# The output projection of a hybrid layer, split into a half that needs mLSTM only and a half that needs attention

## The chip, the cores and the metric

The kernel runs on one core of one Trainium2 chip. A core has five engines that work side by side, each through its own instructions in a fixed order: TensorE (PE; its weight loads are listed as PEld), VectorE (DVE), ScalarE (ACT), GpSimd (POOL), and SyncE (SP), which here only issues DMAs. The metric is the device time of one execution in microseconds (us), lower is better; "before" is the median of three runs.

## The reference, cut to what matters

One layer of an encoder for 2048 + 256 tokens (two request groups, same weights), model width 1024, in float32:

```python
h = rmsnorm(x, norm1_w)
mq, mk, mv, mo, gates, aq, ak, av = split(h @ w_in)
m_out = mlstm_mixer(mq, mk, mv, mo, gates, b_gates, mh_norm_w)   # 8 heads x 64 = 512 channels
a_out = attention_mixer(aq, ak, av, q_norm_w, k_norm_w)          # 8 heads x 64 = 512 channels
x = x + concatenate([m_out, a_out], axis=-1) @ w_out             # (T, 1024) @ (1024, 1024)
h = rmsnorm(x, norm2_w)
u = centred_dwconv(h @ w_up, conv_w, conv_b)
a, g = split(u)
y = rmsnorm(x + (silu(g) * a) @ w_down, final_norm_w)
```

The line with `w_out` is the output projection. Its first 512 input channels come from mLSTM, its last 512 from attention.

## The kernel before, in words

Everything is kept transposed (channels on the 128 partitions, tokens along the free axis), so the 1024 channels are 8 chunks of 128 (`NCC = 8`); the 2304 tokens are 18 tiles of 128 or 9 blocks of 256 (`NB = 9`, `BT = 256`). float32 products are made of three matmuls: each operand is split into a rounded high part (ScalarE's Copy) and the rest (a subtraction on VectorE), and hi x hi, hi x lo, lo x hi are added up in PSUM.

Phase a computes the norm, the attention inputs and the gates. Then two generators run interleaved, `mlstm` and `attention`. Attention goes unit by unit: 512 queries of a head or of two heads against all keys. A unit's matmuls are named by their tiles: `px` (scores for the row maximum, reduced on VectorE into `mx`), `pr` (the negated maximum, spread over partitions; it needs `m` and `m4r` of VectorE), `ps` (the scores), `ph`/`pl` (hi and lo of the exponential, ScalarE and VectorE), `pv` (times the values). When a unit is done, `fin1` to `fin3` copy it out of PSUM (ScalarE), take the reciprocal of the sums (VectorE, tile `rs`), multiply (POOL, tile `o`) and store it with POOL's queue into the DRAM array `mix_d`, 64 channels at a time. fin3 comes in the middle of the next unit. Channel chunks 0 to 3 of `mix_d` come from mLSTM, chunks 4 to 7 from attention; a block's chunk 7 (heads 6 and 7) comes last.

`phase_c` is the output projection, also a generator. It first loads and splits the weights (`weights`, tile `wo`). For block b, `loads` brings the 8 chunks of `mix_d` (tiles `cmx`, split on ScalarE and VectorE) and the residual x (tiles `cx`, four of two channel chunks each). For each z of 0 to 3 `mm` fills one PSUM tile `po` (two output chunks, 8 input chunks x 3 matmuls of 256 columns each, 48 in all; two buffers), and `post` adds it to x on VectorE, stores x1 to DRAM and squares it (ScalarE, summed on POOL). `tail` of the block before, called behind the first `mm` of the next block, makes the mean of squares (tiles `rs_c`, `rcol_c`), multiplies (8 instructions on VectorE, L1020) and stores the normed block into `n2_d`.

`run_both` sets the order in which the program is written down. While mLSTM has steps left, it goes ahead of attention by a fixed ratio. When mLSTM is done, phase_c is created (`after_m`), and from then on each attention step is preceded by one step of phase_c, if the block that phase_c wants is in `g.mixed`, to which attention's fin4 adds a block when its last heads are written. When attention is done, the rest of phase_c's steps is written out between the first steps of the FFN: `n2_sums` (tiles `rn`: sums of n2_d blocks on POOL, stored to `n2t_d`) and `n2_load` (tiles `n` and `nt`, split on ScalarE and VectorE). The first of these take memory that attention used; the later ones take memory that the projection used. Then `up_start` and `phase_d`, the FFN (matmul tiles `pa`, `pb`, `pc` for the up projection, `pd` for down).

Within this order a scheduler places the instructions of each engine: it moves an instruction ahead where its operands are ready earlier in its own model of time, and gives attention's instructions a higher priority (`tc.high_priority(offset=APRI)`) once phase_c runs. Buffers of one tag are used in the order of the program, so with two `po` buffers the third group in the program waits for the first one's addition. On the chip each engine, and each DMA-issuing queue, takes its instructions strictly in the resulting order.

Of the kernel before, what the change touches and what calls it, by code (L numbers as in the profile page):

```python
# [9 lines left out]
F32 = mybir.dt.float32  # L10
F32R = mybir.dt.float32r
AF = mybir.ActivationFunctionType
ALU = mybir.AluOpType
# [4 lines left out]
P = 128  # L18
D = 1024
NCC = D // P  # L20
T1, T2 = 2048, 256
T = T1 + T2
NT = T // P
# [13 lines left out]
BT = 256  # L37
NB = T // BT
NTB = 8
CX = 8  # L40
# [3 lines left out]
WSTEP = 2  # L44
# [2 lines left out]
OW3 = 3  # L47
OTB = 3
MXB = 8
LAGO = 2  # L50
AB = 3
NH = 386
# [3 lines left out]
WB = 8  # L56
# [29 lines left out]
def f32(ap):  # L86
    return ap.bitcast(F32)
# [32 lines left out]
def rstd_bc(g, sp, pp, sqs, n, ptag, name, bufs=1):  # L120


    nc = g.nc
    k = n // P
    ps = pp.tile([P, 512], F32, tag=ptag, name="rs_" + name, bufs=bufs)
    for t in range(k):
        for i, sq in enumerate(sqs):
            nc.tensor.matmul(ps[:, 504 + 2 * t:506 + 2 * t], sq[:, t * P:(t + 1) * P], g.ones, start=i == 0,
                             stop=i == len(sqs) - 1)
    r = sp.tile([P, 4], F32, tag="rcol", name="rcol_" + name)[:, 0:k]  # L130
    nc.vector.tensor_scalar(r, ps[:, 504:504 + 2 * k].rearrange("p (t o) -> p t o", o=2)[:, :, 0], EPS, None, ALU.add)
    nc.gpsimd.tensor_tensor(r, r, g.mhalf[:, 0:k], ALU.pow)
    for t in range(k):
        nc.tensor.matmul(ps[:, t * P:(t + 1) * P], r[:, t:t + 1].to_broadcast([P, P]), g.ident, start=True, stop=True)
    return ps[:, 0:n]
# [824 lines left out]
def phase_c(g, sn, sp, pp, wps):  # L960

    nc = g.nc
    wo = []
    g.normed = set()

    def weights(c):

        wo.append([wps[c // 4].tile([P, 2, 512], F32R, tag="w", name=f"wo{c}_{k}", bufs=WB) for k in range(2)])  # L970
        for k, w in enumerate(wo[c]):
            if c < 4:
                t = g.raw.tile([P, 512], F32, tag="raw", name=f"ro{c}_{k}", bufs=2)
            else:
                t = sp.tile([P, 512], F32, tag="x", name=f"ro{c}_{k}", bufs=CX)
            split(g, w[:, 0, :], w[:, 1, :], g.w_out[0, c * P:c * P + P, 512 * k:512 * k + 512], t)

    def loads(b):
        mx = []
        x = [sp.tile([P, 2, BT], F32, tag="x", name=f"cx{b}_{z}", bufs=CX) for z in range(4)]  # L980
        for z in range(4):
            for o in range(2):
                c = 2 * z + o
                if b % 2:
                    m = sp.tile([P, 2, BT], F32R, tag="mx", name=f"cmx{b}_{c}", bufs=MXB)
                else:
                    m = sn.tile([P, 2, BT], F32R, tag="nT", name=f"cmx{b}_{c}", bufs=NTB)
                nc.sync.dma_start(f32(m[:, 1]), g.mix_d[b, :, c])
                nc.scalar.activation(m[:, 0], f32(m[:, 1]), AF.Copy)  # L989
                nc.vector.tensor_tensor(m[:, 1], f32(m[:, 1]), f32(m[:, 0]), ALU.subtract)  # L990
                mx.append(m)
        for z in range(4):
            for t in range(2):
                nc.sync.dma_start(x[z][:, :, t * P:(t + 1) * P], g.xT[2 * b + t, :, 2 * z:2 * z + 2])
        return x, mx

    def mm(b, z, mx):
        po = pp.tile([P, 2, BT], F32, tag="po", name=f"po{b}_{z}")
        for o in range(2):
            n = slice(((2 * z + o) % 4) * P, ((2 * z + o) % 4 + 1) * P)  # L1000
            for c in range(NCC):
                for k, (a, h) in enumerate(((0, 0), (0, 1), (1, 0))):
                    nc.tensor.matmul(po[:, o], wo[c][z // 2][:, a, n], mx[c][:, h, :],  # L1003
                                     start=(c == 0 and k == 0), stop=(c == NCC - 1 and k == 2))
        return po

    def post(b, z, x, po, acc):
        nc.vector.tensor_tensor(x[z], po, x[z], ALU.add)
        g.st.dma_start(g.x1_d[b, :, 2 * z:2 * z + 2], x[z])
        q = acc if z == 0 else sp.tile([P, 2, BT], F32, tag="sq", name=f"csq{b}_{z}", bufs=1)  # L1010
        nc.scalar.activation(q, x[z], AF.Square, scale=1.0 / 32.0)
        if z:
            nc.gpsimd.tensor_tensor(acc, acc, q, ALU.add)

    def tail(b, x, acc):
        nc.gpsimd.tensor_tensor(acc[:, 0], acc[:, 0], acc[:, 1], ALU.add)
        r = rstd_bc(g, sp, pp, [acc[:, 0]], BT, "r", f"c{b}")
        for z in range(4):
            for o in range(2):
                nc.vector.scalar_tensor_tensor(x[z][:, o], x[z][:, o], g.n2w[:, 2 * z + o:2 * z + o + 1],  # L1020
                                               r, ALU.mult, ALU.mult)
            g.st.dma_start(g.n2_d[:, 2 * z:2 * z + 2, b * BT:(b + 1) * BT], x[z])
        g.normed.add(b)

    for c in range(NCC):
        weights(c)
        if c % WSTEP == WSTEP - 1:
            yield None
    prev = None
    for b in range(NB):  # L1030
        yield 2 * b
        x, mx = loads(b)
        for z in range(4):
            po = mm(b, z, mx)
            if z == 0:
                if prev is not None:
                    tail(*prev)
                acc = sp.tile([P, 2, BT], F32, tag="acc", name=f"cacc{b}", bufs=1)
            post(b, z, x, po, acc)
            if z < 3:  # L1040
                yield None
        prev = (b, x, acc)
    g.c_end = lambda: tail(*prev)

# [111 lines left out]
def phase_d(g, tc, s1, pd, ops, first):  # L1156
# [5 lines left out]
    with ExitStack() as st:  # L1162
# [17 lines left out]
        for b in range(ND):  # L1180
# [70 lines left out]
            def down(nm, acts, wds, order, fin=False):  # L1251

                for (c, z0, z1) in order:
# [73 lines left out]
def body(tc, aps, phases="abcd"):  # L1327
    nc = tc.nc
    g = Ctx()
# [3 lines left out]
    with ExitStack() as st:  # L1333
# [30 lines left out]
        with ExitStack() as s2:  # L1364
# [37 lines left out]
            def after_m():  # L1402
                s_m.close()
                swo = pool(s_wo, "wo", bufs=1, side="right")
                sc = pool(s_wo, "c_s", bufs=2, side="right")
                pc = pool(s_wo, "c_p", bufs=2, space=PSUM, side="right")
                return phase_c(g, g.sn, sc, pc, (sw, swo))

            rest = run_both(g, tc, attention(g, tc, sa, sk, pa), mlstm(g, tc, g.sm, sm2, sw, g.sn, g.pj, pm), after_m)
        with ExitStack() as s2:  # L1410
            s1 = pool(s2, "d_1", bufs=2)
# [13 lines left out]
            first = [up_start(g, s1, pd, ops, 0, NFC)]  # L1425
# [8 lines left out]
def run_both(g, tc, a, m, after_m):  # L1434


    na = 32 * (8 * 2.2 + 1) + 4 * 3.2
    nm = (NT * 6 + 1) + 2 * (NT * 8.7 + 4) + (NT * 5.7 + 4) + NT * OW3
    g.mixed = set()
    c, tile_c = None, None  # L1440
    da = dm = 0.0
    while da is not None or dm is not None:
        if dm is not None and (da is None or dm * na < LEAD * da * nm):
            s = next(m, None)
            dm = None if s is None else dm + s
            if dm is None:
                c = after_m()
                tile_c = next(c)
# [68 lines left out]
```

## Time and profile before

| | |
|---|---|
| runs before | 3471.99 us median of 3 (3470.3 to 3475.37) |
| profiled execution | 3475.05 us, span 3473.3 us, mean granted TensorE clock 0.985 |
| output projection's matmuls (L1003) | 1728, the first at 1388.5 us, the last at 1872.4 us |
| end of attention's matmuls | 1814.9 us |
| FFN's first matmul | 1872.5 us |
| busy | PE 96%, PEld 89%, DVE 77%, ACT 56%, POOL 32% |

Rows of the profile begin with a time from the span's start or with a line of the kernel, then the engine, the operation, the output tiles "<-" the input tiles, and shapes; "x3" is a count, and a bracket at the end gives the idle time of the engine just before and what ended it. SPq is SyncE's queue of DMA issues. DRAM arrays lose a digit in the rows: `n2_d` is n_d and `x1_d` is x_d.

### The profile page before, as it was taken

To read this page: it belongs to the slowest core of one execution; us is meant where nothing else is said; L and a number is where in the kernel's file an instruction comes from. 1 tells how busy PE (TensorE), PEld (TensorE's weight loads), DVE (VectorE), ACT (ScalarE), POOL (GpSimd) and SP (SyncE) were. 2 spreads that over 40 slices of the span, in tenths; PEclk is the share of its full clock that TensorE was granted. 3 is DMA by queue.
4 is the path that set the end of the run, shared out by engine and by line. 5 is a ranking of instruction groups with operands and counts; after the bars stand their busy time and mean duration, and the time that the engine had idled before them with its cause. 6 is when DMAs were issued, how large, how long until landed. Compare 5 with 4: busy or idle time off the path is not lost. (4 is left out here: it accounts for less than half of the span.)

```text
span 3473.3 us, 55765 instructions
## 1 busy us (share of the span) xinstructions
PE 3346.2 (96%) x20058; PEld 3103.0 (89%) x20058; DVE 2670.5 (77%) x4654; ACT 1930.9 (56%) x4329; POOL 1103.9 (32%) x1328
## 2 busy tenths in 40 slices
PE   7989999999999999999988999999999999999998
PEld 6878888888888887987778999999999998999998
DVE  6875687677777789767666888888888878887776
ACT  4536566666666766645554444446544446555555
POOL 6643133222224322211116233225333224322222
PEclk9999999999999999999999999999999999999999
DMA  6765334343355443432218233223333223421221
GB/s 222 238 197 162 117 107 118 104 131 101 105 169 161 131 144 115 145 105 70 68 51 296 73 97 98 74 65 130 127 105 99 67 73 119 145 65 63 73 73 50
DMA packets 258501, 404.29 MB, mean 116 GB/s; under 512 B 33552, under 2 KB 158256, under 8 KB 258224
## 3 DMA queue, kind: packets, MB, share of 16 engines
q1 hardware_dynamic: 230320, 358.24, 32.3%
q0 software_dynamic: 11344, 33.04, 3.5%
q10 hardware_dynamic: 16560, 9.44, 0.9%
q8 instruction: 158, 2.59, 0.3%
q14 instruction: 119, 0.97, 0.1%
HBM read 316.73 MB, written 83.90 MB: 115 GB/s over the span
## 5 line engine op out<-in xcount | busy, mean ns | idle before, releaser
L1257 PE MATMUL pd<-act,wd 128*128 128x384 f32 (+1 forms) x3120 | 593.2, 336 | 25.2 <-DVE acc L1259 14.4
L1257 PEld LDWEIGHTS pd<-act,wd 128*128 128x128 f32 x3120 | 539.5, 189 | 34.0 <-DVE acc L1259 20.0
L586 DVE TENSOR_TENSOR pl<-ps,ph 128x512 fp32r<-128x512 f32 x520 | 354.1, 685 | 235.3 <-ACT ps L585 228.2
L1119 PE MATMUL pa<-nt,wut 128*128 128x386 f32 (+2 forms) x2376 | 454.5, 339 | 2.0 <-DVE nt L1071 2.0
L1119 PEld LDWEIGHTS pa<-nt,wut 128*128 128x128 f32 x2376 | 421.4, 190 | 2.3 <-DVE nt L1071 2.3
L584 ACT ACTIVATE ph<-ps 128x512 fp32r<-128x512 f32 x520 | 309.7, 596 | 177.1 <-PE ps L581 172.3
L558 DVE TENSOR_REDUCE mx<-px 128x1 f32<-128x512 f32 (+1 forms) x528 | 343.8, 671 | 67.4 <-PE px L557 65.4
L1213 DVE SCALAR_TENSOR_TENSOR y<-u,cw,y 128x768 f32<-128x768 f32 (+1 forms) x264 | 314.0, 1190 | 36.3 <-ACT y L1206 29.2
L598 PE MATMUL pv<-ph,v 128*128 128x512 f32 (+1 forms) x1040 | 330.2, 405 | 2.9 <-ACT ph L584 2.4
L1124 POOL TENSOR_TENSOR tw<-ru 128x512 f32<-128x512 f32 x66 | 91.1, 1380 | 744.4 <-DMA ru<-w_up 573.3
L1135 ACT ACTIVATE u<-pa 128x386 f32<-128x386 f32 (+2 forms) x264 | 128.4, 486 | 328.4 <-PE pa L1119 326.9
L585 ACT ACTIVATE ps<-ps 128x512 f32<-128x512 f32 x520 | 310.9, 599 | 0.0
L1259 DVE TENSOR_TENSOR acc<-pd,acc 128x384 f32<-128x384 f32 (+1 forms) x544 | 280.6, 536 | 34.5 <-PE pd L1257 33.5
L1003 PEld LDWEIGHTS po<-cmx,wo 128*128 128x128 f32 x1728 | 233.9, 191 | 32.6 <-ACT cmx L989 16.2
L1003 PE MATMUL po<-cmx,wo 128*128 128x256 f32 x1728 | 242.2, 284 | 14.9 <-ACT cmx L989 14.8
L580 PE MATMUL ps<-qq,kk 128*128 128x512 f32 x520 | 217.0, 421 | 1.8 <-DVE pl L586 1.1
L557 PE MATMUL px<-kk,qq 128*128 128x512 f32 (+1 forms) x528 | 207.7, 411 | 6.6 <-DVE pl L586 3.5
L598 PE MATMUL pv<-pl,v 128*128 128x512 f32 x520 | 206.6, 407 | 6.9 <-DVE pl L586 6.6
L581 PE MATMUL ps<-qm,kl 65*128 65x512 f32 x520 | 209.1, 405 | 0.0
L724 PE MATMUL mj<-mn,wm 128*128 128x256 f32 x1296 | 197.4, 288 | 3.5 <-ACT og L738 2.1
L724 PEld LDWEIGHTS mj<-mn,wm 128*128 128x128 f32 x1296 | 182.1, 192 | 17.6 <-ACT og L738 2.5
L734 PE MATMUL mv<-wm,mn 128*128 128x256 f32 x1296 | 196.2, 288 | 1.1 <-ACT qb L730 0.9
(288 smaller groups left out, 7239.0 us busy)
## 6 DMA issues: line engine op xcount, KB each, us to landing
ru<-w_up SPq DMA_DIRECT2D x132, 512.0 KB, 3.4
mn<-n_d SPq DMA_DIRECT2D x216, 256.0 KB, 3.3
rd<-w_down SPq DMA_DIRECT2D x66, 512.0 KB, 3.6
n_d<-n1T SPq DMA_DIRECT2D x18, 1024.0 KB, 5.6
dm<-nm_d POOLq DMA_DIRECT2D x72, 256.0 KB, 4.0
mjn<-n_d SPq DMA_DIRECT2D x72, 256.0 KB, 3.3
mvn<-n_d SPq DMA_DIRECT2D x72, 256.0 KB, 3.2
q_d<-qz SPq DMA_DIRECT2D x18, 512.0 KB, 3.5
```

Of the source, the lines that this page charges most:

```text
L558: nc.vector.tensor_reduce(s.mx[:, t, z0:z0 + 1], ps[:, 0:w], AX.X, ALU.max)
L580: nc.tensor.matmul(ps, kk[:, kc:kc + P], s.qq[:, 0:N], start=True, stop=False)
L584: nc.scalar.activation(ph, ps, AF.Exp)
L585: nc.scalar.activation(ps, ps, AF.Exp)
L586: nc.vector.tensor_tensor(pl, ps, f32(ph), ALU.subtract)
L598: nc.tensor.matmul(s.pv[0:HD if k in (1, 3) else P, 0:N], v, p, start=(kp == 0 and k == 0), stop=(2 * kp + 2 == s.nk and k == 5))
L724: nc.tensor.matmul(pj[:, o], s.w[c][:, a, o * P:(o + 1) * P], nT[c][:, :, h, :], start=(c + o + k == 0), stop=(c == NCC - 1 and k == 2 and ...
L1003: nc.tensor.matmul(po[:, o], wo[c][z // 2][:, a, n], mx[c][:, h, :], start=(c == 0 and k == 0), stop=(c == NCC - 1 and k == 2))
L1119: nc.tensor.matmul(p, w[:, aa, c, :], ops[k][:, c, bb, 0:n], start=c == 0 and i == 0 and not add, stop=c == NCC // 2 - 1 and i == 2, skip_ ...
L1213: nc.vector.scalar_tensor_tensor(y[:, s:e], u[:, s + k:e + k], cw[:, k, jj:jj + 1], y[:, s:e], ALU.mult, ALU.add)
L1257: nc.tensor.matmul(po, wds[j][c // 4][:, aa, c % 4 * P:(c % 4 + 1) * P], acts[j][:, bb, z0:z1], start=(j == 0 and k == 0), stop=(j == len( ...
L1259: nc.vector.tensor_tensor(accs[c][:, z0:z1], po, accs[c][:, z0:z1], ALU.add)
```

## The change

phase_c becomes two generators. `first` takes channel chunks 0 to 3 (mLSTM's): for each block and each z it loads x (tile `xp`, three buffers), makes a `po` group of 24 matmuls, adds it to x on VectorE and stores the sum into a new DRAM array `xp_d`. `second` takes chunks 4 to 7: it loads `xp_d` back as `cx`, makes a `po` group of 24 matmuls, adds and goes on as before (`post`, `tail`). At the end of phase_c a small loop chooses the program whose step is written down: `second` if its block is in `g.mixed` and `first` has done it, else `first`. `run_both` no longer looks at `g.mixed` and takes one step of this loop per attention step. The loads of a block's chunks (`mixed`) and their splits (`parts`) are separate now, and the first program's loads come half a block ahead.

```diff
-    def loads(b):
-        mx = []
-        x = [sp.tile([P, 2, BT], F32, tag="x", name=f"cx{b}_{z}", bufs=CX) for z in range(4)]
...
+    def mixed(b, c0):
+        mx = []
+        for c in range(c0, c0 + H):
+            if c0:
+                m = sp.tile([P, 2, BT], F32R, tag="mx", name=f"cmx{b}_{c}", bufs=MXB)
+            else:
+                m = sn.tile([P, 2, BT], F32R, tag="nT", name=f"cmx{b}_{c}", bufs=NTB)
+            nc.sync.dma_start(f32(m[:, 1]), g.mix_d[b, :, c])
+            mx.append(m)
+        return mx
+
+    def parts(mx):
+        for m in mx:
+            nc.scalar.activation(m[:, 0], f32(m[:, 1]), AF.Copy)
+            nc.vector.tensor_tensor(m[:, 1], f32(m[:, 1]), f32(m[:, 0]), ALU.subtract)
+
+    def mm(b, z, c0, mx):
+        po = pp.tile([P, 2, BT], F32, tag="po", name=f"po{b}_{z}_{c0}")
...
-            for c in range(NCC):
+            for c in range(H):
...
+    def first():
+        for c in range(H):
+            weights(c)
...
+        mx = mixed(0, 0)
+        parts(mx)
+        for b in range(NB):
+            for z in range(4):
+                x = sp.tile([P, 2, BT], F32, tag="xp", name=f"xp{b}_{z}", bufs=XPB)
+                for t in range(2):
+                    nc.sync.dma_start(x[:, :, t * P:(t + 1) * P], g.xT[2 * b + t, :, 2 * z:2 * z + 2])
+                po = mm(b, z, 0, mx)
+                if b + 1 < NB and z == 1:
+                    nxt = mixed(b + 1, 0)
+                if b + 1 < NB and z == 3:
+                    parts(nxt)
+                    mx = nxt
+                nc.vector.tensor_tensor(x, po, x, ALU.add)
+                g.st.dma_start(g.xp_d[b, :, 2 * z:2 * z + 2], x)
+                yield b + (z == 3)
...
+    def second():
+        for c in range(H, NCC):
+            weights(c)
...
+        prev = None
+        for b in range(NB):
+            mx = mixed(b, H)
+            x = [sp.tile([P, 2, BT], F32, tag="x", name=f"cx{b}_{z}", bufs=CX) for z in range(4)]
+            for z in range(4):
+                nc.sync.dma_start(x[z], g.xp_d[b, :, 2 * z:2 * z + 2])
+            yield b
+            parts(mx)
+            for z in range(4):
+                po = mm(b, z, H, mx)
+                if z == 0:
+                    if prev is not None:
+                        tail(*prev)
+                    acc = sp.tile([P, 2, BT], F32, tag="acc", name=f"cacc{b}", bufs=1)
+                post(b, z, x, po, acc)
+                if z < 3:
+                    yield b
+            prev = (b, x, acc)
+            g.c_end = lambda: tail(*prev)
+            yield b + 1
+
+    s1, s2 = first(), second()
+    done = b = 0
+    while b < NB:
+        if 2 * b in g.mixed and done > b:
+            b = next(s2)
+        elif done < NB:
+            done = next(s1)
+        yield
...
+        dram("xp_d", [NB, P, NCC, BT])
...
             for _ in range(CSTEP):
-                if c is not None and (tile_c is None or tile_c in g.mixed):
-                    tile_c = next(c, NT)
+                if c is not None:
+                    next(c, None)
```

More of the change, by code (lines that the diff above doesn't have):

```diff
@@ L49 @@
 MXB = 8
+XPB = 3
 LAGO = 2
@@ L964, in phase_c @@
     nc = g.nc
-    wo = []
+    wo = {}
     g.normed = set()
+    H = NCC // 2
     def weights(c):
-        wo.append([wps[c // 4].tile([P, 2, 512], F32R, tag="w", name=f"wo{c}_{k}", bufs=WB) for k in range(2)])
+        wo[c] = [wps[c // H].tile([P, 2, 512], F32R, tag="w", name=f"wo{c}_{k}", bufs=WB) for k in range(2)]
         for k, w in enumerate(wo[c]):
-            if c < 4:
+            if c < H:
                 t = g.raw.tile([P, 512], F32, tag="raw", name=f"ro{c}_{k}", bufs=2)
@@ L1005, in mm @@
-        return po
+                    nc.tensor.matmul(po[:, o], wo[c0 + c][z // 2][:, a, n], mx[c][:, h, :],
+                                     start=(c == 0 and k == 0), stop=(c == H - 1 and k == 2))
+        return po
+    def first():
+        for c in range(H):
+            weights(c)
+            if c % WSTEP == WSTEP - 1:
+                yield 0
+        mx = mixed(0, 0)
[14 more added lines that the diff above has]
+                yield b + (z == 3)
@@ L1023, in tail @@
         g.normed.add(b)
[L1025 to L1043, printed above, removed]
+    def second():
+        for c in range(H, NCC):
+            weights(c)
+            if c % WSTEP == WSTEP - 1:
+                yield 0
+        prev = None
[26 more added lines that the diff above has]
+        yield
 OPS = ("11", "21", "t2", "t1", "t3", "22", "t4")
```

22 lines of the change are left out of this document (1 added, 21 removed).

## The prediction

> **What bounds the kernel now.** I read the page first, then the stretches around the output projection, then the order of time on TensorE, VectorE and the DMA queue where a stretch shows a gap.
>
> ```profile
> span 3473.3 us, 55765 instructions
> PE 3346.2 (96%) x20058; PEld 3103.0 (89%) x20058; DVE 2670.5 (77%) x4654; ACT 1930.9 (56%) x4329; POOL 1103.9 (32%) x1328
> L1003 PE MATMUL po<-cmx,wo 128*128 128x256 f32 x1728 | 242.2, 284 | 14.9 <-ACT cmx L989 14.8
> ```
>
> TensorE (PE) is the bound, and the edit neither adds nor removes one of its 1728 projection matmuls: only PE's idle time, its clock and the waits at the two ends of the projection can change. They lie in these stretches (columns: stretch, length, busy time and count of PE, PEld, DVE, ACT, POOL; then granted clock, DMA share, GB/s):
>
> ```profile
> core 0: us, PE busy (x) PEld busy (x) DVE busy (x) ACT busy (x) POOL busy (x), PEclk, DMA share, GB/s
> 1565.18:1569.71 4.53, 0.48 (x5) 0.17 (x3) 4.44 (x12) 0.00 (x0) 0.00 (x0) 1.00 0.39 130
> 1569.71:1577.35 7.64, 7.64 (x22) 5.92 (x23) 2.67 (x4) 5.16 (x10) 0.00 (x0) 0.55 0.68 198
> 1577.35:1598.30 20.95, 18.68 (x74) 11.86 (x72) 16.94 (x27) 12.90 (x26) 2.40 (x3) 1.00 0.10 26
> 1600.00:1640.00 40.00, 40.00 (x268) 35.99 (x267) 24.79 (x42) 21.24 (x43) 6.97 (x7) 1.00 0.19 60
> 1814.90:1829.02 14.12, 0.19 (x2) 0.00 (x1) 6.52 (x13) 1.60 (x3) 2.39 (x3) 0.66 0.66 187
> 1829.02:1872.53 43.51, 43.51 (x351) 43.51 (x351) 21.40 (x30) 13.24 (x20) 32.65 (x30) 0.95 0.94 322
> ```
>
> With projection work at hand PE issues 268 matmuls in 40 us; without it 74 in 20.95 us, where VectorE (DVE) is 81% busy. So there are "gated stretches" in which attention runs alone, and at attention's end 14.1 us in which PE stands. In PE's order of time (start, duration, count):
>
> ```profile
> 1562.04 0.41 PE L1003 MATMUL po<-cmx,wo 128*128 128x256 f32 x2
> 1569.71 0.33 PE L569 MATMUL pr<-identr,m4r 128*128 128x128 f32 x1 [4.05 <-DVE m4r L566]
> 1577.58 1.10 PE L598 MATMUL pv<-ph,v 128*128 128x512 f32 x4
> 1598.32 0.50 PE L1003 MATMUL po<-cmx,wo 128*128 128x256 f32 x2 [0.30 <-ACT cmx L989]
> 1814.60 0.48 PE L598 MATMUL pv<-pl,v 128*128 128x512 f32 x1
> 1829.02 29.12 PE L1003 MATMUL po<-cmx,wo 128*128 128x256 f32 x228 [13.93 <-ACT cmx L989]
> 1862.13 10.56 PE L1003 MATMUL po<-cmx,wo 128*128 128x256 f32 x86
> 1872.53 2.29 PE L1119 MATMUL pa<-n,wu 128*128 128x386 f32 x12
> 1878.92 0.34 PE L1119 MATMUL pc<-nt,wut 128*128 128x386 f32 x1
> ```
>
> From these the issue interval of a matmul: 256 columns (10.56 - 0.28)/85 = 0.121 us, 512 columns (1.10 - 0.39)/3 = 0.237 us, 386 columns (2.29 - 0.34)/11 = 0.177 us.
>
> **The change: the order it makes.** The compiled order of both kernels is the same up to the first projection matmul and again from early in the FFN on, so 1388 to about 1960 us is all there is to cost. The two programs do not run apart there: one step of the projection is handed out per attention step, and by the time it is wanted block b's attention is always emitted, so the order alternates: first half of block 0, second half of block 0, first half of block 1, and so on to block 8. The first program is never more than one block ahead. Since both halves take their turns in the same two po buffers, two second-half groups that wait for attention's last chunk (channel chunk 7 of mix_d) hold both, and no later first half can pass them. What the order does give is 72 matmuls (the first half of one block, 96, less the 24 fewer that are issued early from the waiting second half), moved once from behind attention's end to ahead of it. There are 342 projection matmuls behind the last attention matmul before, 271 after. Counting 512-column attention matmuls between the last early projection matmul and the first that uses chunk 7, the three gated stretches (blocks 4, 5, 6) have 96, 106, 108 before and 80, 104, 108 after. Only the first shrinks.
>
> **Step 1, the gated stretch of block 4.** It lasts from 1562.3 to 1598.3, 36.0 us. Its 4.05 us gap is VectorE's:
>
> ```profile
> 1566.16 3.21 DVE L1020 SCALAR_TENSOR_TENSOR cx<-cx,nw,rs_c 128x256 f32<-128x256 f32 x8
> 1569.29 0.16 DVE L564 TENSOR_REDUCE m<-mx 128x4 f32<-128x16 f32 x1
> 1814.89 3.22 DVE L1020 SCALAR_TENSOR_TENSOR cx<-cx,nw,rs_c 128x256 f32<-128x256 f32 x8 [3.25 <-PE rs_c L134]
> 1818.03 3.37 DVE L615 RECIPROCAL rs<-rs 64x128 f32<-64x128 f32 x4
> 1877.43 1.49 DVE L1071 TENSOR_TENSOR nt<-nt 128x772 fp32r<-128x772 f32 x1
> ```
>
> The eight multiplications of block 3's tail() stand in front of the row maximum that pr waits for. In the new order they stand behind it, and some 20 projection matmuls (2.4 us) lie between the last px and pr, so I take the gap as gone, and with it the low clock after it (0.55 over 7.64 us, so 7.64 x 0.45 = 3.4 us). The new length: 72 x 0.121 = 8.7 us of moved work, 16 x 0.237 = 3.8 us for the 16 attention matmuls that now run beside it, and 80 matmuls at the gated pace of 20.95/74 = 0.283 us, 22.7 us: 35.2 us. VectorE's 3.2 us of tail work now falls into the gated part; there it has 4.0 us to spare in 20.95, so the addition is 0 to 3.2, and I take 1.6, the middle. 36.8 against 36.0: attention's end moves **+0.8** us (-0.8 to +2.4).
>
> The Trainium skill (TensorE: Matmul & The Clock Gate, Part 1) says that an idle window of about 3.4 us halves the array clock and a busy window of the same length restores it. By that the dip is half of 3.4 us, 1.7 instead of 3.4, and the saving and the sum would be 1.7 us worse; the trace's 0.55 over 7.64 us agrees with the halving, not with so short a recovery.
>
> **Step 2, the wait at attention's end.** The chain before: VectorE's tail of block 6 and then the reciprocal (rows above), POOL's product, its store to mix_d, SP's load of the chunk, its split.
>
> ```profile
> 1810.82 0.71 POOL L132 TENSOR_TENSOR rcol_c<-rcol_c,mhalf 128x2 f32<-128x2 f32 x1 [6.87 <-DVE rcol_c L131]
> 1823.08 1.14 POOL L622 DMA_DIRECT2D mix_d<-o  x2 [0.29 <-POOL o L619]
> 1826.05 0.34 SPq L988 DMA_DIRECT2D cmx<-mix_d  x1
> 1826.43 2.04 SPq L1086 DMA_DIRECT2D rn<-n_d  x4
> 1828.52 2.24 SPq L1069 DMA_DIRECT2D n<-n_d  x4
> 1872.72 1.40 SPq L1069 DMA_DIRECT2D nt<-n2t_d  x3
> rn<-n_d SPq DMA_DIRECT2D x8, 386.0 KB, 5.1
> x_d<-cx SPq DMA_DIRECT2D x9, 256.0 KB, 4.7
> ```
>
> After, the same chain with two differences. The mean's small instructions (rcol_c on VectorE, the power on POOL, two rs_c matmuls) come behind the last pl instead of ahead of it; POOL's power took 0.71 us, and for the two small steps around it I estimate 0.5, so the reciprocal starts 1.2 us later. And the eight loads (rn, n) stand ahead of the chunk's on SP, their splits ahead of its split on ScalarE and VectorE. The loads wait for PE and VectorE, not for the mix; the reload of x ahead of them waits for a store to land (4.7 us in the median of this stretch, row x_d<-cx), one that is issued a little ahead of attention's end, so by estimate they start 3.3 us behind it. They carry 8 x 386 KB = 3.16 MB, at 322 GB/s 9.8 us: done 13.1 us behind it. The chunk's load, 1826.05 - 1814.9 = 11.2 us behind attention's end before, is now at 11.2 + 1.2 = 12.4; for the 0.7 us in which the eight are still under way I add 0.6. **+1.8** us; bounds 0 (all hidden, the mean too) and 13 (second rival).
>
> **Step 3, behind the wait.** 342 matmuls took 43.5 us. After, 71 of them are gone, 8.6 us, and 16 FFN matmuls stand among the rest, 16 x 0.177 = 2.8: 37.7 us, -5.8. The 2.8 us of FFN work come to nothing: the nt loads go into memory that the last projection matmul frees (issued 1872.72, 0.2 us behind it), their split starts at 1877.43, pc at 1878.92, 6.4 us behind the projection's end; work done before then only leaves a longer wait. So **-5.8** us (-8.6 if the 2.8 do count, -3.0 if FFN's other operands, read 8.6 us sooner, are late by 2.8).
>
> **Step 4, what is added.** 36 VectorE additions at the price of this row, 36 x 0.682 = 24.6 us, and 36 stores and 36 reloads of 256 KB (36 x 0.33 + 36 x 0.46 = 28 us of SP's issue, 18.9 MB):
>
> ```profile
> L1008 DVE TENSOR_TENSOR cx<-po,cx x36: 665/682/692, 1407.2 to 1874.2; 128x512 f32<-128x512 f32 x36
> L994 SPq DMA_DIRECT2D cx<-xT x64: 367/460/1889, 1393.7 to 1732.3; - x64
> ```
>
> The cover: beside full PE work VectorE is busy 24.8 of 40 us, and the DMA engines 19%. A po group is now 24 matmuls, 2.9 us alone, and with two buffers its addition must be done within the next group's 2.9 us or PE stands. Behind a reload on SP, which waits for its store to land (that same 4.7 us), stand other reloads, xT loads and the next mix chunks, all a z-step (3 to 6 us) ahead of need; no chunk-7 load is directly behind one. Bounds 0 and 24.6; I take **+1.5**, near the lower, since the row of 1600 to 1640 has the room. Weights, splits, xT loads and squares keep their count: 0.
>
> **The sum:** 0.8 + 1.8 - 5.8 + 1.5 = -1.7 us. The profiled execution took 3475.05 us (span 3473.3 and 1.75 around it), 3.06 above the median 3471.99 of the three runs. So 3473.3 for that execution, and **3470** as a median.
>
> **The rivals.**
> No loss, a real gain (faster): the chunk is as early as before (step 2: 0), additions cost nothing (0), the FFN work counts (-8.6) and block 4's stretch takes its best (-0.8): -9.4, 3462.6. For it: the FFN's first loads start some 10 us sooner behind attention's end. Against it: the nt loads do not.
> The loads ahead of the chunk (slower): if the eight loads go only when SP gets there at 1826, because their buffers or the reload ahead of them come late, the chunk is issued 4.3 us later and lands up to 9.8 us later still, +13 in place of +1.8: 3470 + 11 = 3481. It decides from about 11 us on, in place of the 1.8. For it: ScalarE and VectorE, too, now split these loads before the chunk. The Trainium skill (DMA: Bandwidth & Descriptors, Queues, rings and completion order) says that each DMA engine takes a row's descriptors in ring order, so a late chunk would indeed wait behind all 3.16 MB. Against it: they wait for no part of the mix.
> Additions that show (slower): half of the 24.6 us comes to light as waits for a po buffer, or for a reload on SP: +11, 3481.
> The program does run ahead (faster): the 14.1 us gap and the gated stretches fill, -20 or more, 3450. The compiled order excludes it but for mistakes of mine.
>
> **How the numbers follow.** What a measurement of this kernel can tell from no change is about 0.2%, 7 us. My forecast with no more than that either way: 0.40. Faster: the real gain 0.23 and the program ahead 0.02, 0.25. Slower: loads ahead 0.17, additions 0.18, 0.35. The range: 3458 (the gain, and the execution's own scatter of some 4 us) to 3488 (a slower rival, with half of the other's price); the forecast's own is 3464 to 3478.
>
> **What would show it.** In the profile after: pr of block 4's stretch with no 4 us wait, and the granted clock near 1 there; the stretches of blocks 5 and 6 as before; a wait of po for the chunk of 14 to 17 us (14.1 before); the projection ending some 38 us behind it; the wait of pc for nt longer. Wrong if po waits for additions (VectorE or PSUM) sum to more than 5 us, if the wait for the chunk is over 20 us, or if matmuls of a later block stand in a gated stretch.

## The result, and the profile after

The changed kernel takes 3485.05 us, median of 5 runs (3484.16 to 3489.82), beside 3470.30 of the kernel before in the same series (3469.56 to 3475.37): a ratio of 1.0041, 95% interval 1.0027 to 1.0056. It is 14 us slower where 1.7 us faster, and no measurable change, was forecast. The profiled execution took 3489.82 us, the slowest of the five; the profile of the kernel before is of an execution of 3475.05 us, near the top of its range too.

The page's lines of the changed kernel:

```profile
span 3488.1 us, 55875 instructions
PE 3347.9 (96%) x20058; PEld 3097.7 (89%) x20058; DVE 2700.1 (77%) x4690; ACT 1932.0 (55%) x4329; POOL 1112.3 (32%) x1328
L1003 PE MATMUL po<-cmx,wo 128*128 128x256 f32 x1728 | 244.4, 283 | 17.2 <-ACT cmx L994 15.0
```

TensorE's busy time is the same to 2 us; the rest of the 14.8 us between the two spans is idle time. To place them I follow three marks in PE's order of time: the first projection matmul, the last attention matmul (attention's end) and the end of the span. Changed kernel, PE:

```profile
1828.89 0.40 PE L599 MATMUL pv<-pl,v 128*128 128x512 f32 x1
1844.90 0.80 PE L1003 MATMUL po<-cmx,wo 128*128 128x256 f32 x2 [15.05 <-ACT cmx L994]
1846.79 22.84 PE L1003 MATMUL po<-cmx,wo 128*128 128x256 f32 x172 [1.09 <-DVE cmx L995]
1884.21 1.59 PE L1158 MATMUL pb<-n,wu 128*128 128x386 f32 x8
1897.69 1.01 PE L129 MATMUL rs_c<-ones,cacc 128*128 128x2 f32 x4 [9.62 <-POOL cacc L1039]
```

| | before | after | difference |
|---|---|---|---|
| first projection matmul | 1388.5 | 1390.7 | +2.2 |
| from there to attention's end (1815.1, 1829.3) | 426.6 | 438.6 | +12.0 |
| from there to the end of the span | 1658.2 | 1658.8 | +0.6 |

The 2.2 us lie where both orders are the same; the first projection matmul of the kernels below scatters from 1384.0 to 1393.1 us, without a pattern. So nearly all of the loss is in the 427 us in which attention and projection share TensorE, and behind attention's end, where 71 projection matmuls (8.6 us) were taken away, nothing was won. The stretch from the first projection matmul to attention's end, before and then after (columns as in the prediction):

```profile
1388.50:1815.10 426.60, 408.64 (x2443) 346.01 (x2441) 293.07 (x515) 235.59 (x464) 64.65 (x68) 0.98 0.28 85
1390.70:1829.30 438.60, 418.25 (x2512) 351.72 (x2511) 313.00 (x542) 235.21 (x460) 63.88 (x68) 0.98 0.39 121
```

Most of the 12.0 us are busy time of TensorE, as the profile models it, 9.6 us more, of which the 71 moved matmuls are 8.6; idle time grew by 2.4. So the moved work was paid ahead of attention's end and not hidden there. Behind it TensorE is busy 7.3 us less and idle 7.9 us more, and its waits from attention's end to 1960 us show for what. Changed kernel (engine, line, what it waited for, us in total, times, longest):

```profile
PE po L1003 <- ACT cmx L994: 15.0, 1, 15.0
PE rs_c L129 <- POOL cacc L1039: 9.6, 1, 9.6
PE po L1003 <- DVE cmx L995: 1.1, 1, 1.1
PE pc L1158 <- ACT u L1174: 0.7, 1, 0.7
```

The kernel before, from 1814 us on:

```profile
PE po L1003 <- ACT cmx L989: 13.9, 1, 13.9
PE pa L1119 <- DVE wu L1116: 2.0, 1, 2.0
PE pa L1119 <- DVE nt L1071: 2.0, 1, 2.0
```

26.4 us of waits against 17.9, in a window that is some 15 us shorter: 8.5 us more, for 8.6 us of work less.

In the attention stretch, the gated stretches (from the last early projection matmul to the first that uses attention's chunk 7; columns as in the prediction) are, in the kernel before and then in the changed one:

```profile
1562.16:1598.32 36.16, 29.82 (x116) 20.46 (x114) 26.83 (x48) 19.31 (x38) 3.12 (x4) 0.91 0.25 73
1641.84:1678.63 36.79, 31.39 (x121) 20.70 (x119) 28.25 (x50) 19.93 (x39) 2.61 (x4) 0.95 0.25 72
1722.20:1760.56 38.36, 32.99 (x124) 23.17 (x122) 29.15 (x52) 20.62 (x40) 3.12 (x4) 0.87 0.21 62
```

```profile
1581.61:1609.56 27.95, 23.09 (x91) 13.98 (x89) 23.21 (x41) 18.36 (x37) 2.41 (x3) 1.00 0.32 95
1653.84:1692.76 38.92, 33.01 (x114) 22.00 (x113) 28.93 (x52) 21.55 (x42) 2.41 (x3) 0.87 0.25 79
1736.86:1775.49 38.63, 32.50 (x119) 21.18 (x118) 30.87 (x54) 22.27 (x44) 2.41 (x3) 0.91 0.24 76
1829.85:1844.90 15.05, 0.00 (x1) 0.00 (x1) 11.92 (x16) 4.47 (x7) 7.90 (x8) 0.67 0.81 278
1844.90:1884.38 39.48, 38.39 (x295) 38.09 (x296) 20.66 (x31) 10.70 (x19) 24.79 (x24) 0.91 0.96 330
```

The first one is 8.2 us shorter and at full clock, but it begins 19.5 us later, and the second is 2.1 us longer. That second one scatters: the kernels below that have the order of before show 36.8 to 39.1 us for it.

### The profile page after: what moved, and what is told of

Same layout as the page of the kernel before. It is cut to its first block, busy times and chain, and to the rows that moved or that the text cites. A ratio compares the mean times of both kernels' runs of the same rounds, so it can differ in the third digit from the quotient of the medians.

```text
span 3488.1 us, 55875 instructions
## 1 busy us (share of the span) xinstructions
PE 3347.9 (96%) x20058; PEld 3097.7 (89%) x20058; DVE 2700.1 (77%) x4690; ACT 1932.0 (55%) x4329; POOL 1112.3 (32%) x1328
## 4 chain that ended last, share of the span: by engine, by line
PE 72%; DVE 12%; DMA 6%; ACT 3%; issue 3%; POOL 2%; SPq 0%; POOLq 0%; DVEq 0%; ACTq 0%
PE pa L1158 12%; PE pd L1296 11%; PE pv L599 9%; PE pc L1158 6%; PE mj L725 4%; PE mv L735 4%; PE po L1003 4%; PE ps L581 3%; PE ps L582 3%; PE px L558 3%; PE pb L1158 3%; PE mN L867 2%; PE mv L751 2%; PE mj L751 1%; DVE y L1252 1%
```

## The experiments

After the first reading I held two theories with rivals. **A:** behind attention's end the FFN's preparation paces (loads, sums, weights), so that matmuls moved from behind that point to ahead of it are paid in full and never won back; rival **P:** TensorE paces there. **B:** block 8's own second half makes the new 9.6 us wait. For the attention stretch: **C**, the round trip of x through DRAM; **D**, the 36 additions; and later **E**, VectorE standing at the splits of late chunks with attention's row maxima behind it; rival **F**, the order of the matmuls itself.

All runs in one table: matmuls ahead of attention's end against before (from the compiled order), the two stretches of each profiled execution, and the ratio to the kernel before of the same series. Four kernels have the order of before up to attention's end (before, less_behind, dma_more, sums_dve): 426.6 to 428.2 us there, which is the scatter of that column. The next column holds one execution each as well, and executions of the kernel before differ by 6 us among five, so a few us in it are not read alone.

| kernel | ahead | first po to attention's end | attention's end to span's end | ratio (95%) |
|---|---|---|---|---|
| before | 0 | 426.6 | 1658.2 | 1 |
| changed | +71 | 438.6 | 1658.8 | 1.0041 (1.0027 to 1.0056) |
| last_whole | +71 | 438.0 | 1656.8 | 1.0035 (1.0022 to 1.0047) |
| kept | +63 | 438.4 | 1656.0 | 1.0021 (1.0013 to 1.0030) |
| two_groups | +15 | 429.1 | 1656.4 | 1.0004 (0.9995 to 1.0012) |
| round_trip | -5 | 453.8 | 1660.1 | 1.0085 (1.0072 to 1.0098) |
| less_behind | 0 | 427.3 | 1648.2 | 0.9990 (0.9981 to 0.9999) |
| less_ahead | -96 | 428.8 | 1652.9 | 0.9999 (0.9990 to 1.0007) |
| own_po | +159 | 440.0 | 1649.5 | 1.0034 (1.0022 to 1.0047) |
| dma_more | 0 | 427.2 | 1666.4 | 1.0033 (1.0021 to 1.0046) |
| parts_pool | +69 | 437.7 | 1661.9 | 1.0034 (1.0022 to 1.0046) |
| kept_own | +87 | 446.5 | 1660.8 | 1.0057 (1.0045 to 1.0070) |
| kept_own_pool | +87 | 434.9 | 1663.4 | 1.0058 (1.0046 to 1.0070) |
| sums_dve | 0 | 428.2 | 1658.0 | 1.0007 (0.9998 to 1.0015) |
| all_pool | +71 | 435.5 | 1661.7 | 1.0041 (1.0028 to 1.0053) |
| own_all_pool | +159 | 435.1 | 1654.7 | 1.0016 (1.0007 to 1.0024) |
| kept_all_pool | +63 | 429.1 | 1653.8 | 1.0004 (0.9995 to 1.0013) |
| before_all_pool | -2 | 429.4 | 1659.1 | 1.0006 (0.9997 to 1.0015) |
| last2_whole | 0 | 424.5 | 1657.4 | 0.9994 (0.9985 to 1.0003) |
| last3_whole | -10 | 429.0 | 1656.1 | 1.0013 (1.0004 to 1.0022) |

### The new wait behind attention's end: last_whole

```diff
...
-                po = mm(b, z, H, mx)
+                po = mm(b, z, H, mx) if b < NB - 1 else mm(b, z, 0, g.mx8 + mx, NCC)
...
```

> The changed kernel, but block 8 is not split: its four groups have 48 matmuls, its residual comes from xT, no reload and no second addition for it. Theory A (what follows attention's end is paced by the preparation of the FFN: loads, sums on POOL, weights; matmuls moved ahead of attention's end are lost there): the wait of rs_c for the sum, 9.6 us in the changed kernel, stays at 7 us or more, 3483 to 3487. Theory B (block 8's own second half, its reload and its late addition, makes that wait): the wait falls below 3 us, 3475 to 3479.

3484.31 us. The wait did fall; PE's waits of this kernel from 1800 to 1930 us:

```profile
PE po L1003 <- ACT cmx L994: 13.9, 1, 13.9
PE pa L1162 <- ACT u L1178: 3.1, 1, 3.1
PE rs_c L129 <- POOL cacc L1039: 1.5, 1, 1.5
PE pc L1162 <- DVE nt L1114: 1.4, 1, 1.4
```

rs_c waits 1.5 us in place of 9.6, as B has it, but the kernel is hardly faster, as A has it: other operands of the FFN are late instead, in part. Theory B falls as the cause of the time. The chain that ended last in the changed kernel, from attention's end to that wait, names what is behind it: the FFN's sums (rn), their store, the next weights into the memory that the sums held (ru), the weights' sums (tw), and only then the sum of squares:

```profile
1840.20 1.62 POOL rn L1129
...
1849.96 5.53 DMA rn<-n_d
...
1858.69 5.05 DMA n2t_d<-rn
1863.81 4.92 DMA ru<-w_up
...
1892.88 1.68 POOL tw L1166
1894.56 1.67 POOL cacc L1036
1896.31 1.33 POOL cacc L1039
1897.69 1.01 PE rs_c L129 x4
```

### Who paces behind attention's end: less_behind, dma_more, sums_dve

```diff
-            for c in range(NCC):
+            for c in range(NCC if b < NB - 1 else NCC // 2):
...
```

> The kernel before, with the products of chunks 4 to 7 left out for block 8: 96 matmuls (11.6 us of TensorE) fewer, all behind attention's end; loads and everything else stay. Theory A (behind attention's end the FFN's preparation paces, not TensorE): no more than 3 us faster, the distance from attention's end to the kernel's end stays within 3 us of 1650. Rival P (TensorE paces there): 9 to 11.6 us faster.

> The kernel before, with three copies of 1 MB from DRAM to DRAM (9 us at the 340 GB/s of this stretch) issued right behind the load of chunk 7 of block 7, ahead of the loads of the FFN's preparation. Theory A: 7 to 11 us slower, though no matmul waits for the copies. Rival P: 0 to 3 us slower.

```diff
+        if b == 7:
+            for k in range(3):
+                nc.sync.dma_start(g.more_d[k], g.mix_d[7])
...
```

> The kernel before, with the 16 sums of the FFN's preparation (rn, 0.9 to 1.6 us each on POOL) on VectorE. If POOL paces the preparation behind attention's end: 3 to 6 us faster. If the traffic paces it (DMA engines 0.85 to 1.02 busy there): within 2 us. If VectorE gets too late with po's additions: 2 to 5 us slower.

```diff
-            todo = [lambda c=c: n2_sums(g, s1, 0, c) for c in range(NCC // 2)]
+            todo = [lambda c=c: n2_sums(g, s1, 0, c, ("vector",) * 4) for c in range(NCC // 2)]
```

less_behind, with 11.6 us less of TensorE's work, is 3.5 us faster by the ratio (0.3 to 6.6); its one profiled execution is 10 us shorter behind attention's end, and eleven executions do not bear that out. So about a third comes back, a little over A's bound and far from P's. dma_more is 11.5 us slower (0.33%) though no matmul waits for its copies: A. The loads behind the copies take longer from issue to landing (the last figure); dma_more, and then before:

```profile
n<-n_d SPq DMA_DIRECT2D x6, 386.0 KB, 10.7
```

```profile
n<-n_d SPq DMA_DIRECT2D x6, 386.0 KB, 6.6
```

For the rn loads it is 8.3 us against the 5.1 in the prediction's row. The Trainium skill (DMA: Bandwidth & Descriptors, Queues, rings and completion order) says that each DMA engine consumes the descriptors of a row's ring in order; by that, loads issued behind 3 MB of copies come later, and these rows agree with it. The first sum on POOL starts 24.9 us behind dma_more's attention's end (1813.7), where before it was 15.3 (1830.41 against 1815.1), but not all of these 9.6 us are the loads': in dma_more's order the sum stands behind a sum of squares.

```profile
1837.33 1.29 POOL L1016 TENSOR_TENSOR cacc<-cacc,csq 128x512 f32<-128x512 f32 x1 [14.52 <-ACT csq L1014]
1838.58 0.87 POOL L1093 TENSOR_TENSOR rn<-rn 128x386 f32<-128x386 f32 x1
```

sums_dve takes the rn sums off POOL and is not faster, so these sums alone are not what paces, unless VectorE pays as much for them. The preparation's transfers remain, with the DMA engines 0.96 busy and 330 GB/s in the last row of the windows above (0.94 and 322 before); so does POOL's other work, the sums of weights (tw) and of squares (cacc), which sums_dve leaves where it was and which fills the last stretch of the chain above, to 1897.7. Which of them decides was not separated.

### Is the work ahead of attention's end paid in full: less_ahead, own_po, two_groups

```diff
-            for c in range(NCC):
+            for c in range(NCC if b != 1 else NCC // 2):
...
```

> The kernel before, with the products of chunks 4 to 7 left out for block 1: 96 matmuls (11.6 us) fewer, all ahead of attention's end, where TensorE has no idle time. Theory A: attention's end 8 to 11.6 us earlier and the kernel as much faster. If work taken from ahead of attention's end only lengthens the gated stretches of blocks 4 to 6: less than 4 us.

> The changed kernel, with a po buffer for each of the two programs (one each, in place of two shared): first halves pass second halves that wait, so 159 projection matmuls more than before are done ahead of attention's end (71 in the changed kernel), 183 behind it, and of the three gated stretches one is left. Theory A: the 159 add 19.2 us ahead of attention's end, the two filled stretches give back 8 to 14 of it, nothing comes back behind it: 3476 to 3484, no faster than before. Rival P: 3462 to 3470.

```diff
-        po = pp.tile([P, 2, BT], F32, tag="po", name=f"po{b}_{z}_{c0}")
+        po = pp.tile([P, 2, BT], F32, tag=f"po{c0}", name=f"po{b}_{z}_{c0}", bufs=1)
```

> The kernel before, but each group of 48 matmuls is two of 24, each added to x on VectorE: 36 additions of 0.68 us more, one program, x in SBUF, order nearly that of before (15 matmuls move ahead of attention's end, 1.8 us). Theory D: 3475 to 3480. Theory A and C: 3470 to 3474.

```diff
...
+            po = mm(b, z, mx, 0)
+            nc.vector.tensor_tensor(x[z], po, x[z], ALU.add)
+            po = mm(b, z, mx, NCC // 2)
```

less_ahead refutes A's second half as I had put it: 96 matmuls (11.6 us) less there gave nothing (0.9999). The projection caught up with attention sooner and a fourth gated stretch came up, of 31 us. So that stretch is not paced by the sum of TensorE's work: what is taken away can come back as waiting. own_po is the other side of it: the program now runs ahead, one gated stretch is left of three, 159 matmuls are done early, and the kernel is no faster than the changed one. 19.2 us of moved work made attention's end 13.4 us later, so filling two stretches gave back some 6 us, and behind attention's end 1658.2 became 1649.5 in the profile, less than half of the 19.2. two_groups, the additions alone, costs 1.4 us (-1.7 to 4.2) with 1.8 us of moved work in it; 3474.68 us lies between the two forecasts, and D falls as the cause of 14 us. Its first gated stretch is short as well (27.4 us, beginning 11.1 us later than before), so this needs neither the second program nor the round trip.

### Where attention's 12 us come from: kept, round_trip, parts_pool, all_pool, kept_all_pool

> The changed kernel, but x stays in SBUF between the two halves: no store into xp_d and no reload (36 of each, 18.9 MB less), all 36 additions stay. Theory C (the round trip costs, by SyncE's queue or by the traffic): 3476 to 3480. Theory D (the 36 additions on VectorE cost) and theory A (the 72 matmuls moved ahead of attention's end are not won back behind it): 3482 to 3487.

```diff
-                x = sp.tile([P, 2, BT], F32, tag="xp", name=f"xp{b}_{z}", bufs=XPB)
+                x = sp.tile([P, 2, BT], F32, tag="x", name=f"cx{b}_{z}", bufs=CX)
...
-                g.st.dma_start(g.xp_d[b, :, 2 * z:2 * z + 2], x)
...
-                nc.sync.dma_start(x[z], g.xp_d[b, :, 2 * z:2 * z + 2])
```

> The kernel before, but x goes from xT into a tile, from there into xp_d and back into its tile: 36 stores and 36 loads of 256 KB more, no addition, groups of 48. Theory C: 3475 to 3480. Theory A and D: 3469 to 3472.

```diff
+            g.st.dma_start(g.xp_d[b, :, 2 * z:2 * z + 2], xp)
+        for z in range(4):
+            nc.sync.dma_start(x[z], g.xp_d[b, :, 2 * z:2 * z + 2])
```

kept is 4 us faster than the changed kernel (7 by the ratios), between the theories, and its attention stretch is as long. round_trip is 29 us slower than before; there the reload stands right behind its store, so it prices a worse round trip than the change has. At the issues that the round trip added, SyncE's queue stood, from 1388 to 1825 us of the changed kernel, for:

```profile
SPq L1027 <- DVE xp L1026: 54.3, 14, 7.5
SPq L1059 <- DMA xp_d<-xp: 33.8, 20, 3.4
SPq L1019 <- DMA xp_d<-xp: 13.6, 8, 2.6
```

These 102 us are no price by themselves. Summed over all rows of its attention stretch the queue stands 322 us, in the kernel before 327, and in kept, without the round trip, 356: it stands at other issues instead. What did change is that chunks of mix_d, which come through the same queue, are late for their splits. ScalarE, which begins a split, waited for their loads, in the changed kernel and then before:

```profile
ACT cmx L994 <- DMA cmx<-mix_d: 74.7, 27, 16.2
```

```profile
ACT cmx L989 <- DMA cmx<-mix_d: 27.3, 18, 4.5
```

In kept it is still 65.4 us, so the round trip does not make them late alone, and what does was not shown. VectorE shows the consequence. Its order of time in the changed kernel:

```profile
1464.63 0.42 DVE L995 TENSOR_TENSOR cmx<-cmx 128x256 fp32r<-128x256 f32 x1 [5.16 <-ACT cmx L994]
1464.98 0.68 DVE L1031 TENSOR_TENSOR cx<-po,cx 128x512 f32<-128x512 f32 x1
1465.58 3.21 DVE L1043 SCALAR_TENSOR_TENSOR cx<-cx,nw,rs_c 128x256 f32<-128x256 f32 x8
1468.71 0.69 DVE L559 TENSOR_REDUCE mx<-px 128x1 f32<-128x512 f32 x1
```

VectorE stands 5.2 us at the split of a chunk that has not come, and an addition, a tail and attention's row maxima queue behind it. In sum over the stretch, changed kernel and then before:

```profile
DVE cmx L995 <- ACT cmx L994: 22.9, 16, 5.2
```

```profile
DVE cmx L990 <- ACT cmx L989: 6.4, 11, 1.4
```

That is theory E. It is about the place of these waits, ahead of attention's row maxima: in all, VectorE waits no longer than before in the stretch (121 us, 132 before). Its tests move the subtraction of the splits to POOL, in the second program (parts_pool) or in both (all_pool), the latter also with x kept (kept_all_pool), with own po buffers (own_all_pool), and in the kernel before (before_all_pool); the cut of all_pool:

```diff
-            nc.vector.tensor_tensor(m[:, 1], f32(m[:, 1]), f32(m[:, 0]), ALU.subtract)
+            nc.gpsimd.tensor_tensor(m[:, 1], f32(m[:, 1]), f32(m[:, 0]), ALU.subtract)
```

> The changed kernel, with the subtraction that splits the second program's chunks (attention's, 36 in all) on POOL in place of VectorE. Theory E (VectorE stands at these splits, 22.9 us in the changed kernel against 6.4 before, because the chunks come late, and attention's row maxima stand behind them): VectorE's wait for cmx falls below 8 us, attention's end comes 4 to 8 us earlier, 3476 to 3481. Rival F (the wait is idle time that VectorE would have had anyway; the order of the matmuls costs): attention's end within 2 us, 3483 to 3487.

> The changed kernel, with the subtractions that split the mix chunks of both programs on POOL; the matmuls ahead of attention's end are as many as in the changed kernel (71 more than before). Theory E (VectorE stands at the splits, attention's maxima behind it; with only the second program's splits moved, the wait at the first's took its place, 18.5 us): VectorE waits for no cmx, attention's end 8 to 12 us earlier than in the changed kernel, 3473 to 3478. Rival F (the order of the matmuls costs): attention's end within 2 us, 3483 to 3487.

> The changed kernel with x kept in SBUF and all splits on POOL. Theory E: 6 to 10 us faster than x kept alone (3481): 3471 to 3475. Rival F: 3479 to 3483.

> The changed kernel with a po buffer for each program and all splits on POOL. Theory E: 6 to 10 us faster than own po buffers alone (3482): 3472 to 3476. Rival F: 3480 to 3484.

> The kernel before, with all splits of the mix chunks on POOL; VectorE waits 6.4 us for them before. Theory E: 1 to 4 us faster than before. Rival F: within 1 us; slower, if the splits hold POOL and attention's products (o) come late, which moves attention's chunk 7.

parts_pool told nothing: the first program's splits took over the wait (18.5 us). all_pool misses its forecast: VectorE waits for no split any more, attention's stretch is 3.1 us shorter, and the kernel is as slow as the changed one. Only both together help:

| first po to attention's end (ratio) | splits on VectorE | splits on POOL |
|---|---|---|
| x through DRAM | 438.6 (1.0041) | 435.5 (1.0041) |
| x kept in SBUF | 438.4 (1.0021) | 429.1 (1.0004) |

kept_all_pool has 63 matmuls (7.6 us) more ahead of attention's end than before and needs 2.5 us more; it takes 3473.91 us beside 3473.56. So in the attention stretch neither the round trip nor VectorE's splits alone is the cause: take away one and the other holds most of the loss. The ratios, over all runs, agree for the splits, which alone give nothing; the round trip alone gives about half of the loss back. own_all_pool is 6 us faster than own_po by the ratios, at E's lower bound; before_all_pool is not faster than before, so the gain is not one that POOL would give anyway.

### Towards a better version: kept_own, kept_own_pool, last2_whole, last3_whole

> The changed kernel with x kept in SBUF between the halves and a po buffer for each program: 87 matmuls more than before ahead of attention's end (10.5 us), one gated stretch of 74 attention matmuls left of three. From the runs of x kept (3481) and of own po buffers (3482): two filled stretches give 8 to 14 us back, 3470 to 3478. If gated stretches cost nothing and only the work moved counts: 3481 or more.

> The same with the second program's splits on POOL; no gated stretch of over 70 attention matmuls is left. Theory E: 4 to 8 us faster than the same without POOL. Rival F: within 2 us of it.

Both are 20 us slower than before, and by the medians (3494.75 and 3494.73) E's 4 to 8 us are missed. In the profiles kept_own_pool's attention stretch is 11.6 us shorter than kept_own's, but its profiled execution, 3486.05 us, is the fastest of five and 8.7 us below its median, so this can be a difference of executions. Both lose behind attention's end (1660.8, 1663.4), where block 8's first halves now stand among block 7's second ones; this wasn't followed further.

The last two put the moved matmuls back behind attention's end and keep the rest of kept_all_pool:

```diff
...
-        for b in range(NB):
+        for b in range(NB - 2):
...
-                po = mm(b, z, H, mx)
+                po = mm(b, z, 0, mx, NCC) if whole else mm(b, z, H, mx)
...
```

> The changed kernel with x kept in SBUF, all splits on POOL, and blocks 7 and 8 not split (groups of 48): 342 projection matmuls stand behind attention's end, as before the change, 63 (7.6 us) more than with blocks 7 and 8 split; the first gated stretch stays short (78 attention matmuls against 96 before). Theory A (work ahead of attention's end costs its length, work behind it is covered): 5 to 8 us faster than the same with blocks 7 and 8 split (3473.9), 3466 to 3469, which is 2 to 5 us faster than before. Rival P: within 2 us of it.

> The same with block 6 whole too: 352 matmuls behind attention's end. Theory A: as the one with two whole blocks, within 2 us. Rival P: 1 to 3 us slower than that.

last2_whole has 63 matmuls fewer ahead of attention's end than kept_all_pool, a stretch 4.6 us shorter (424.5, the shortest of all), 3.6 us more behind it in the profile, and a ratio of 0.9994 against 1.0004: 3.5 us, between A (5 to 8) and P (under 2). At 3470.74 beside 3472.36 us it can't be told from the kernel before; last3_whole is 4.5 us slower by its ratio. No version here that does all of the work beats the kernel before by more than can be measured.

## Why the prediction was wrong, step by step

**Step 1, attention's end: +0.8 said, +12.0 measured. This step failed.** What it said of block 4's gap is right: pr has no wait in the new stretch, and the granted clock there is 1.00. Its sum says that nearly all of the moved work is hidden where attention runs alone; in the profile TensorE is 9.6 us busier up to attention's end. Two terms were too small.

First, the stretch should have begun 12.5 us later (8.7 + 3.8); with the 2.2 us of the start taken off it began 17.3 us later, 4.8 too late. With x kept alone it is 17.6, with the splits on POOL alone 15.9, and with both 12.4, as worked out: so the step left out the lateness that the round trip and VectorE's standing at the splits make together.

Second, its gated part should have been 24.3 us (22.7 + 1.6) and was 28.0. Late splits are not the reason, for with all splits on POOL it is still 27.4 to 27.9 us (kept_all_pool, all_pool). The term was mis-sized: the 74 matmuls in 20.95 us are 70 of 512 columns and 4 small ones, so the 80 of 512 columns take 0.299 us each, 23.9 us, and with the whole 3.2 us of VectorE's tail in place of half, 27.1.

Block 5's stretch, "unchanged", grew by 2.1 us, which the scatter of kernels with the order of before covers. The cover that step 4 claimed, "all a z-step (3 to 6 us) ahead of need", failed for the chunks: their loads come late, and VectorE's place in the order is spent waiting. The prediction looked for that only as a wait of po or at chunk 7, and named po's waits as the sign; po waited 0.9 us for an addition in the whole stretch, and the wait for the chunk stayed below its 20 us. The sign was on VectorE and ScalarE.

**Step 2, the wait at attention's end: +1.8 said, +2.0 measured** (15.05 against 14.12, and 1.09 for the second split). Right; the rival with the eight loads ahead of the chunk did not happen.

**Step 3, behind the wait: -5.8 said.** The projection itself did end sooner: 39.5 us behind the wait for 43.5, -4.0, or -5.1 without the 1.09 already counted. But the step took this for time won, and here it failed too: PE's waits grew by 8.5 us, and from attention's end to the end of the span the time is the same to 0.6 us. The step had noted that pc waits for its operands, and allowed for 2.8 us of it; it should have asked what the FFN waits for in general. In the trace of before two rows that it quoted pointed there: DMA engines 0.94 busy behind the wait, and pc 6.4 us behind the last projection matmul.

**Step 4, additions and reloads: +1.5 said.** The additions alone: 1.4 us, right. The round trip was mis-sized: leaving it out gives 4 us by the medians and 7 by the ratios, more only together with the splits. It comes due in step 1. By which wait it is paid is not shown: SyncE's queue stands no longer in all, and in the attention stretch no addition on VectorE waits for a reload.

**The rivals.** "Additions that show" came out near the measured time (3481), by luck: up to attention's end po waited 0.9 us for additions, and no addition waited for a reload. By luck too 3485 lies within the stated range, whose upper end (3488) was made from rivals that did not act. "The program does run ahead", priced at 3450, was run as own_po: two of three gated stretches filled, and it took 3482, because the price left out that work done early is paid for ahead of attention's end.

**What stays open.** Of the 12.0 us, 9.5 go with x kept and splits on POOL together (1.0 of it for 8 matmuls fewer ahead); what makes the chunks late, and through which waits the one delay holds the loss when the other is gone, was not resolved. About a third by the middle of less_behind's ratio, and at most 6.6 of 11.6 us, of TensorE's work taken from behind attention's end comes back as time; which part of the preparation decides was not separated.

## What to carry to other kernels

Work that is moved from behind a synchronisation point to ahead of it is only won if TensorE paces behind that point: look at what the next stage waits for there, and count those waits with the moved work taken out. The price of a late operand can stand on the engine that prepares it, here VectorE and ScalarE, and not as a wait of TensorE for it. The standing of a queue at new issues is a price only if its standing in all has grown: sum all of its rows before calling it one. And where two causes delay the same chain, an experiment that removes one of them can show little; remove both before the theory is dropped.

## What the runs showed of the hardware

Behind the 15.05 us wait the granted clock stayed at 0.50 for 6.8 us, and behind the 9.6 us wait for rs_c it was back after less than that (stretches of 3.4 us of the changed kernel, columns as before):

```profile
1844.90:1848.30 3.40, 2.31 (x9) 2.01 (x10) 2.99 (x3) 0.42 (x1) 3.32 (x4) 0.50 0.92 292
1848.30:1851.70 3.40, 3.40 (x18) 3.40 (x18) 2.18 (x4) 1.72 (x4) 1.19 (x2) 0.50 0.93 357
1851.70:1855.10 3.40, 3.40 (x30) 3.40 (x30) 0.69 (x1) 0.71 (x2) 0.94 (x1) 0.96 0.90 231
1897.69:1901.10 3.41, 3.41 (x12) 3.41 (x13) 2.10 (x3) 0.90 (x2) 3.41 (x3) 0.50 1.05 405
1901.10:1904.50 3.40, 3.40 (x16) 3.40 (x15) 0.69 (x1) 1.37 (x3) 2.66 (x2) 0.69 0.26 105
```

The Trainium skill (TensorE: Matmul & The Clock Gate, Part 1), of which the prediction spoke, has a recovery after one busy window of about 3.4 us and calls the window free-running. Here the first 3.4 us behind the long wait are themselves part idle (2.31 us busy of 3.40), and the clock came back behind the second, the full ones. Behind the shorter wait the work is full from its start, and the clock was low for 3.41 us and, at 0.69 between 0.50 and 1.00, for some 0.62 of the next 3.40: about 5.5 us. With 0.55 over 7.64 us, about 6.9 us at 0.50, after the 4.05 us gap before, these three low clocks are of one and a half to two windows of 3.4 us, which is the size to reckon with here. That a window must be wholly busy to count would fit all three; it is a reading of these rows, which no run tested by itself.
